# Attention and the first quarter of the output projection in one written order on five engines, with map sums and sub-norm roots on GpSimd

## The chip, the cores and the metric

The kernel runs on one core of one Trainium2 chip. The metric is the device time of one execution in microseconds, the median of several runs. The core has five engines that run side by side, each through its own list of instructions in order: TensorE (PE; its weight loads are shown as PEld), VectorE (DVE), ScalarE (ACT), GpSimd (POOL) and SyncE (SP), which here only issues DMA transfers. An instruction that waits for another engine or a transfer holds up everything behind it in its engine's list.

## What is computed

One layer of a diffusion backbone in fp32: 512 latent tokens and 256 context tokens of width 2048. The part that matters here:

```
p = modulate(rmsnorm(x)) @ w_in                       # one input projection for both mixers
q_da, k_da, v_da        = heads of p                  # 8 differential heads, two halves of 64
c_q, c_kv, k_rope       = rest of p                   # compressed inputs of 8 latent heads
w  = softmax(q1 k1^T) - lambda * softmax(q2 k2^T)     # differential head: two maps, 768 keys
o_da = rmsnorm_per_head(w @ v) * subln_w * (1 - lambda_init)
q, k, v = c_q @ w_uq, c_kv @ w_ukv                    # latent heads
o_mla = softmax([q_nope,q_rope] [k_nope,k_rope]^T * scale) @ v
x = x + g1 * (concat(o_da, o_mla) @ w_o)
x = x + g2 * conv_ffn(modulate(rmsnorm(x)))           # the longest stage, not touched here
out = rmsnorm(x) * final_w
```

## The kernel before

All matrix products are made in a split form: an fp32 operand is copied to a rounded high part (ScalarE, `sc.copy`) and a low part, the difference (VectorE, `ve.tensor_tensor`), and `mm3` (lines 101 to 106) adds three products high*high, high*low, low*high. Every weight block and every intermediate operand thus needs a ScalarE and a VectorE step before TensorE can use it.

Stages, in the order of the program: normalisation and modulation; the input projection (features, then values, line 483 on, whose results are split and written to DRAM by lines 496 to 498, the second half of them from GpSimd's queue); the eight differential heads (`da_head`, line 551); the eight latent heads (loop at line 657, with `latent_pair` at 591 projecting queries, keys and values for two heads); the output projection in four groups (g = 0 to 2 at line 735, the fourth in a later written order); the MLP; the final norm.

A differential head: `da_queries` (539) projects the head's queries, 48 matmuls of 512 columns, turns them by the rotary table (`apply_rope`) and stacks high and low parts. Keys and values come back from DRAM (554 to 558). For each of four query tiles and two maps `scores_softmax` (506) makes four matmuls into a two-bank score tile `s` (two buffers), VectorE takes the row maximum (512), ScalarE the exponent with its row sum (514). The two maps are joined: GpSimd scales the second map (567), VectorE scales the first and adds (568):

```
gp.tensor_scalar(out=ps[1], in0=ps[1], scalar1=rl[:, 1:2], scalar2=neglam, op0=ALU.mult, op1=ALU.mult)
ve.scalar_tensor_tensor(out=ps[0], in0=ps[0], scalar=rl[:, 0:1], in1=ps[1], op0=ALU.mult, op1=ALU.add)
```

`weighted_values` (517) then does six times: four transposes of the joined map into `pt`, high and low parts `wth` and `wtl` (line 80 and 81, by `split_tiles`), `mm3` into `po`; a copy (525) ends the head.

A latent head has 40 score matmuls, scales its map on VectorE (668) and uses the same `weighted_values`. `sub_norm` (646) is called once in each latent head for one stored differential head: load, square, a sum over partitions by a full fp32 matmul with ones (653), the root by `rstd` (157: two ScalarE and four VectorE steps), and a scaling (655).

What sets the order: the first stage and everything from the fourth projection group on stand in an order written out by hand (`tc.manual_schedule`). Between them, and so in all that is described here, the program gives operations and their dependences, and the framework's scheduler puts each engine's instructions in an order of its own; it mixes, for instance, the next head's query matmuls into the present head's scores, and the first output projection matmuls into the last latent head. Buffers come from pools; a tile that takes the place of an older one waits until that one's users are done.

Of the kernel before, what the change touches and what calls it, by code (L numbers as in the profile page):

```python
# [13 lines left out]
ALU = mybir.AluOpType  # L14
# [38 lines left out]
def layer_kernel(ctx: ExitStack, tc: tile.TileContext, small, rope, c_row, cc_row, x_t, ctx_t, ada, ada_k,  # L53
# [72 lines left out]
    ones32 = cst.tile([P, P], F32, name="ones32")  # L126
# [379 lines left out]
    def scores_softmax(mms, pool, tag, bufs, l):  # L506
        s = s_tile()
        for c0, c1 in ((0, T), (T, TT)):
            for i, (a, b) in enumerate(mms):
                pe.matmul(s[:, c0:c1], a, b[:, c0:c1], start=i == 0, stop=i == len(mms) - 1)  # L510
        m = sm.tile([P, 1], F32, tag="m", name=nm("m"), bufs=4)
        ve.tensor_reduce(out=m, in_=s[:, :TT], axis=AX.X, op=ALU.max, negate=True)
        p = pool.tile([P, TT], F32, tag=tag, name=nm(tag), bufs=bufs)
        sc.activation(p, s[:, :TT], AF.Exp, bias=m, accum_out=l)
        return p

    def weighted_values(pool, ws, v, dst, last=False):
        po = b_tile("po", 1)
        for kt in range(NKEY):
            pt = b_tile("f", 2) if last and kt % 3 else b_tile("pt", 1)  # L520
            for qt in range(NQT):
                pe.transpose(pt[:, qt * P:(qt + 1) * P], ws[qt][:, kt * P:(kt + 1) * P], ident)
            wth, wtl = split_tiles(pool, ("wth", "wtl"), [P, T], 2, pt)
            mm3(po, v(kt), (wth, wtl), kt == 0, kt == NKEY - 1)
        sc.copy(dst, po)


    da = tc.alloc_tile_pool(name="da", bufs=1, reuse_waits="tile")

# [6 lines left out]
    def da_rtmp():  # L536
        return da.tile([P, T], F32, tag="rt", name=nm("rt"), bufs=2)

    def da_queries(h):
        if h == 0:  # L540
            qs = [da.tile([P, T], F32R, tag=f"qs{i}", name=nm("qs"), bufs=2) for i in range(2)]
            for i in range(2):
                nc.sync.dma_start(qs[i].bitcast(F32), q0_d[i])
            return qs
        lat = b_tile("f", 2)
        feature(lat, None)
        q = da_rtmp()
        apply_rope(q, lat, da_rtmp)
        return stacked_queries(da, q, DA_SCALE)

    def da_head(h, qs):
# [5 lines left out]
        v = da.tile([P, 2, NKEY, P], F32R, tag="v", name=nm("v"), bufs=2)  # L557
        nc.sync.dma_start(v.bitcast(F32), v_d[h // 4][h % 4])
        ws = []
        for qt in range(NQT):  # L560
            c = slice(qt * P, (qt + 1) * P)
            l = sm.tile([P, 2], F32, tag="l", name=nm("l"), bufs=4)
            ps = [scores_softmax([(qs[i][:, c], ks[:, i]), (qs[i][:, c], kl[:, i])], da, f"p{i}", (8, 3)[i],
                                 l[:, i:i + 1]) for i in range(2)]
            rl = sm.tile([P, 2], F32, tag="rl", name=nm("rl"), bufs=4)
            ve.reciprocal(rl, l)
            gp.tensor_scalar(out=ps[1], in0=ps[1], scalar1=rl[:, 1:2], scalar2=neglam, op0=ALU.mult, op1=ALU.mult)
            ve.scalar_tensor_tensor(out=ps[0], in0=ps[0], scalar=rl[:, 0:1], in1=ps[1], op0=ALU.mult, op1=ALU.add)
            ws.append(ps[0])
        o = da.tile([P, T], F32, tag="o", name=nm("o"), bufs=2)  # L570
        weighted_values(da, ws, lambda kt: (v[:, 0, kt], v[:, 1, kt]), o)
        nc.sync.dma_start(o_d[h], o)

    for h in range(NH):
        da_head(h, da_queries(h))
    ap_.release()


    mc = tc.alloc_tile_pool(name="mc", bufs=1, side="right", reuse_waits="tile")

    def latents(src, width):
        hl = [mc.tile([P, width], F32R, name=nm("cn")) for _ in range(2)]
        for i in range(2):
            nc.sync.dma_start(hl[i].bitcast(F32), src[i])
        return hl

    cqn = [latents(d, T) for d in cq_d]
    ckvn = [latents(d, TT) for d in ckv_d]
    ma = tc.alloc_tile_pool(name="ma", bufs=1, side="right", reuse_waits="tile")

    def latent_pair(pr):

        pool = mb if pr % 2 else ma
        wh, wl = wblock(w_uqr[pr], 384)
        po = b_tile("f", 2)
        for j in range(3):
            mm3(po, (wh[:, j * P:(j + 1) * P], wl[:, j * P:(j + 1) * P]), cqn[j], j == 0, j == 2)
        qr = ma.tile([P, T], F32, tag="qr", name=nm("qr"), bufs=1)
        apply_rope(qr, po, lambda: ma.tile([P, T], F32, tag="rt", name=nm("rt"), bufs=2))
        qs = stacked_queries(pool, qr, MLA_SCALE, 1)  # L600
        qn, kn, vs = [], [], []
        qw = wblock(w_uqn[pr], 768)
        kw = wblock(w_ukv[pr])

        def queries_keys(i):
            po = b_tile("f", 2)
            for j in range(3):
                o = i * 384 + j * P
                mm3(po, [w[:, o:o + P] for w in qw], cqn[j], j == 0, j == 2)
# [804 lines left out]
```

## Time and profile before

| what | value |
|---|---|
| median of 3 runs | 2440.16 us (2439.8 to 2440.46) |
| span of the profiled execution | 2439.6 us |
| TensorE busy | 2367.0 us, 97% |
| VectorE busy | 1735.5 us, 71% |
| ScalarE busy | 1117.0 us, 46% |
| GpSimd busy | 220.2 us, 9% |
| mean granted TensorE clock | 0.992 |
| first query matmul of the differential heads | 473.99 us after the span's start |
| last matmul of the first projection group | 919.3 us |

The profile is one execution, and its span lies 0.56 us under the median of the runs. A row of a stretch gives its length and then, for PE, PEld, DVE, ACT and POOL, busy time and number of instructions, then the granted clock, the share of the DMA engines and GB/s. A row of the order of time gives start, duration, engine, line, output<-inputs, sizes, and in brackets the idle time before it with what ended it. A row of groups gives line, engine, names, shapes, count, busy time, mean ns of one, and the idle time before. A wait row gives who waited for whom: total us, times, longest.

### The profile page before, as it was taken

The page shows a single profiled execution, that of the slowest core. Times are in us where ns is not written, and L with a number is a line of the kernel's source. Part 1 is how long each engine was busy: PE and PEld are TensorE (multiplying, and loading weights), DVE is VectorE, ACT ScalarE, POOL GpSimd, SP SyncE. Part 2 cuts the span into 40 slices and gives each one's busy share as a digit, 9 for nine tenths or more (in the row PEclk, how much of TensorE's full clock was granted, in tenths as well). Part 3 has the DMA queues.
Part 4 walks back from the last instruction along what each step waited for, and adds up shares of the span by engine and source line. Part 5 has one row for each costly group of instructions (what it writes and reads, how often), then busy time and mean ns, then how long its engine had stood idle before and what let it go on. Part 6 is the DMA issues. An engine that isn't in the chain of part 4 may idle for free.

```text
span 2439.6 us, 32889 instructions
## 1 busy us (share of the span) xinstructions
PE 2367.0 (97%) x12758; PEld 1978.4 (81%) x12758; DVE 1735.5 (71%) x2316; ACT 1117.0 (46%) x1696; POOL 220.2 (9%) x244
## 2 busy tenths in 40 slices
PE   6999999999999999999999999999999999999998
PEld 3678877777777778889888888888888888888888
DVE  6668876388868878378667676767666666666667
ACT  4432121155646542245445454545454545454545
POOL 0000000121100003100111111111111111111110
PEclk9999999999999999999999999999999999999999
DMA  8758889555411149423555555555555565556573
GB/s 300 279 211 309 327 319 330 181 166 144 127 59 44 44 161 349 146 87 113 147 130 143 134 140 137 137 139 136 141 134 143 132 143 132 141 135 140 133 188 111
DMA packets 130707, 403.32 MB, mean 165 GB/s; under 512 B 14323, under 2 KB 25075, under 8 KB 122099
## 3 DMA queue, kind: packets, MB, share of 16 engines
q1 hardware_dynamic: 104118, 350.87, 43.7%
q0 software_dynamic: 25280, 49.30, 11.6%
q8 instruction: 100, 1.64, 0.3%
q10 hardware_dynamic: 1152, 1.05, 0.1%
q14 instruction: 57, 0.47, 0.1%
HBM read 331.68 MB, written 69.48 MB: 164 GB/s over the span
## 4 chain that ended last, share of the span: by engine, by line
PE 76%; DVE 8%; issue 7%; ACT 4%; DMA 3%; POOL 2%; SPq 0%; DVEq 0%; ACTq 0%; POOLq 0%
PE y L1133 11%; PE b L105 9%; PE b L104 9%; PE b L106 9%; PE z L1133 5%; PE y L1135 5%; PE s L104 3%; PE s L105 3%; PE s L106 3%; PE z L1135 3%; PE s L510 3%; PE x L1133 2%; DMA ada<-in_ada 2%; PE b L206 1%; PE f L104 1%
## 5 line engine op out<-in xcount | busy, mean ns | idle before, releaser
L989 DVE TENSOR_TENSOR wl<-wr,wh 128x1024 fp32r<-128x1024 f32 x144 | 176.4, 1225 | 157.8 <-ACT wh L981 157.1
L981 ACT CAST wh<-wr 128x1024 fp32r<-128x1024 f32 x144 | 151.0, 1049 | 234.0 <-PE b L105 118.5
L104 PE MATMUL b<-ah,wh 128*128 128x512 f32 (+1 forms) x664 | 256.8, 387 | 0.0
L105 PE MATMUL b<-al,wh 128*128 128x512 f32 (+1 forms) x664 | 256.7, 387 | 0.0
L106 PE MATMUL b<-ah,wl 128*128 128x512 f32 (+1 forms) x664 | 255.9, 385 | 0.0
L1154 POOL DMA_DIRECT2D x_d<-xs x160 | 139.6, 1004 | 1162.6 <-ACT xs L1153 1159.3
L989 DVE TENSOR_TENSOR wl<-rb,wh 128x1024 fp32r<-128x1024 f32 x123 | 150.0, 1220 | 126.9 <-ACT wh L981 126.8
L981 ACT CAST wh<-rb 128x1024 fp32r<-128x1024 f32 x123 | 129.2, 1050 | 185.7 <-PE b L105 116.1
L989 DVE TENSOR_TENSOR wl<-ws,wh 128x1024 fp32r<-128x1024 f32 x123 | 150.1, 1220 | 90.1 <-ACT wh L981 90.1
L80 ACT CAST wh<-wr 128x1024 fp32r<-128x1024 f32 (+3 forms) x102 | 99.2, 972 | 217.0 <-PE b L106 62.1
L171 DVE CUSTOM_DVE_ANT_0 ada<-ada,cb,smt 128x2048 f32<-128x2048 f32 x64 | 152.5, 2382 | 54.6 <-DMA ada<-in_ada 54.2
L981 ACT CAST wh<-ws 128x1024 fp32r<-128x1024 f32 x123 | 128.2, 1043 | 130.3 <-DVE ws L943 44.3
L1133 PE MATMUL y<-a2k,wh 128*128 128x512 f32 x656 | 164.0, 392 | 0.0
L81 DVE TENSOR_TENSOR wl<-wr,wh 128x1024 fp32r<-128x1024 f32 (+3 forms) x102 | 116.9, 1146 | 62.1 <-ACT wh L80 61.7
L104 PE MATMUL b<-a2k,wh 128*128 128x512 f32 (+1 forms) x376 | 141.6, 377 | 5.9 <-ACT a2k L838 4.3
L106 PEld LDWEIGHTS b<-ah,wl 128*128 128x128 f32 x664 | 124.8, 188 | 25.7
L104 PEld LDWEIGHTS b<-ah,wh 128*128 128x128 f32 x664 | 125.1, 188 | 22.9
L105 PEld LDWEIGHTS b<-al,wh 128*128 128x128 f32 x664 | 125.1, 188 | 21.9
L105 PE MATMUL b<-a2k,wh 128*128 128x512 f32 (+1 forms) x376 | 140.8, 374 | 0.0
L106 PE MATMUL b<-a2k,wl 128*128 128x512 f32 (+1 forms) x376 | 140.0, 372 | 0.0
L1133 PEld LDWEIGHTS y<-a2k,wh 128*128 128x128 f32 x656 | 118.6, 189 | 21.6
L1133 PE MATMUL y<-b2k,wh 128*128 128x512 f32 x410 | 107.8, 393 | 0.0
(454 smaller groups left out, 5757.2 us busy)
## 6 DMA issues: line engine op xcount, KB each, us to landing
ada<-in_ada SPq DMA_DIRECT2D x64, 1024.0 KB, 6.4
rb<-in_w_up SPq DMA_DIRECT2D x123, 512.0 KB, 4.3
wr<-in_w_dn SPq DMA_DIRECT2D x88, 512.0 KB, 4.3
x_d<-xs POOLq DMA_DIRECT2D x160, 256.0 KB, 6.0
wr<-in_w_up SPq DMA_DIRECT2D x53, 512.0 KB, 4.2
wr<-in_w_f SPq DMA_DIRECT2D x34, 512.0 KB, 6.0
ada<-in_ada SPq DMA_DIRECT2D x32, 512.0 KB, 6.4
adak<-in_ada_k SPq DMA_DIRECT2D x32, 512.0 KB, 6.3
```

Of the source, the lines that this page charges most:

```text
L80: sc.copy(dst_h, src)
L81: ve.tensor_tensor(dst_l, src, dst_h.bitcast(F32), op=ALU.subtract)
L104: pe.matmul(out, st[0], mv[0], start=start, stop=False, **kw)
L105: pe.matmul(out, st[0], mv[1], start=False, stop=False, **kw)
L106: pe.matmul(out, st[1], mv[0], start=False, stop=stop, **kw)
L171: ve.tensor_tensor_reduce(out=junk, in0=w, in1=vec, op0=ALU.mult, op1=ALU.add, scale=1.0, scalar=col("b_ada", j), accum_out=dst[:, j:j + 1])
L510: pe.matmul(s[:, c0:c1], a, b[:, c0:c1], start=i == 0, stop=i == len(mms) - 1)
L981: sc.copy(t, raw[:, k * n_:k * n_ + n_])
L989: ve.tensor_tensor(t, raw[:, k * n_:k * n_ + n_], hi[k].bitcast(F32), op=ALU.subtract)
L1133: pe.matmul(o, w[j][0], hs[j], start=start and j == 0, stop=False, skip_group_check=True)
L1135: pe.matmul(o[:, h0], w[j][1], hs[j][:, h0], start=False, stop=j == 7, skip_group_check=True)
L1154: gp.dma_start(x1_d[dt], x, accum_op=ALU.add)
```

## The change

The differential heads, the latent heads and the first projection group (g = 0) are recorded as steps with a time (`at(t, f)`), sorted by it and issued under `tc.manual_schedule` for all five engines, GpSimd included. The times only decide the order in each engine's list. `SPANS` gives each head its length: 17, six of 23.2 and 19 us for the differential heads, 21 and 22.8 in turn (the last 16) for the latent ones; `BASE` are their starts, and the last projection step stands at 399.1.

- Within a head, scores are spread evenly; the next head's query matmuls run from 6 us before the head at an even pace; the weighted values of head h run inside head h + 1, one key block every 3.05 us (2.5 to 3.3 in the latent heads).
- The joining of the maps: GpSimd scales the second map as before, ScalarE scales the first (`da_first`), GpSimd adds them (`da_sum`). VectorE no longer takes part.
- `sub_norm`: the square is split into two parts (ScalarE, GpSimd) and summed by two matmuls with fp32r ones; the root's four VectorE steps and the last scaling go to GpSimd (five steps, in `power`) and ScalarE (`root`, and the scaling by `subs`).
- Pools: a new pool `dp` holds maps, transposed parts, values and head outputs for both kinds of heads, opened ahead of `da`; the values of a head are two tiles; stored outputs live in a pool `mq` that takes the place of `da`.
- The first projection group and its weight blocks, with the split of the 16 head outputs, follow in the same order; the loads of the next group's first blocks too. The modulation rows of the groups g = 1 and 2 (`next_gemv`) are as before, behind the written order.

The core of the diff (`...` marks what is left out):

```diff
+    def at(t, f, *a):
+        plan.append((t, len(plan), f, a))
...
+    def block(t, key, src, cols=1024):
+        at(t - 12, fetch, key, src, cols)
+        at(t - 3.4, high_part, key)
+        at(t - 2.2, low_part, key)
...
-    def scores_softmax(mms, pool, tag, bufs, l):
+    def softmax(t, key, mms, tag, bufs, l, tall):
+        at(t, score, key, mms)
+        at(t + tall + 0.1, peak, key)
+        at(t + tall + 1.2, exponent, key, tag, bufs, l)
+        return t + tall + 2.4
...
+    def weighted_values(t, h, step, dst, done=None):
         for kt in range(NKEY):
+            t0 = t + step * kt
+            at(t0, turn, h, kt)
+            split_at(t0 + 0.55, (dp, dp), ("wth", "wtl"), [P, T], 2, lambda: live["pt", h],
+                     lambda hl, kt=kt: live.__setitem__(("wt", h, kt), hl), width=0.7)
+            at(t0 + step - 0.2, values, h, kt)
...
+    SPANS = [17, 23.2, 23.2, 23.2, 23.2, 23.2, 23.2, 19] + [21, 22.8, 21, 22.8, 21, 22.8, 21, 16]
+    BASE = [sum(SPANS[:i]) for i in range(17)]
...
+    def da_first(h, qt):
+        p = live[("s", h, qt, 0), "p"]
+        sc.mul(p, p, live["rl", h, qt][:, 0:1])
+
+    def da_sum(h, qt):
+        p, p1 = (live[("s", h, qt, i), "p"] for i in range(2))
+        gp.tensor_tensor(out=p, in0=p, in1=p1, op=ALU.add)
+        live["w", h, qt] = p
...
+    FIRST = -9.0
+    at(FIRST, first_queries)
+    at(FIRST, load_keys, 0)
...
+    for h in range(NH):
+        b, step = BASE[h], SPANS[h] / 8
         for qt in range(NQT):
+            for i in range(2):
+                t = softmax(b + (2 * qt + i) * step, ("s", h, qt, i), ...)
+            at(t, da_norm, h, qt)
+            at(t + 0.2, da_second, h, qt)
+            at(t + 0.2, da_first, h, qt)
+            at(t + 1.5, da_sum, h, qt)
+        at(b + 2, load_values, h)
+        if h + 1 < NH:
+            at(b + 1, load_keys, h + 1)
+            f0, pace = (FIRST, 0.75) if h == 0 else (b - 6, (SPANS[h] - 0.3) / 16)
...
+            for kt in range(KT):
+                at(f0 + pace * kt, da_feature, h + 1, kt)
...
+        weighted_values(BASE[h + 1] + 4.8, h, 3.05 if h < 7 else 2.7, ...)
...
+        def low_():
+            live["sub", "lo"] = tile_("s2", F32R)
+            gp.tensor_tensor(out=live["sub", "lo"], in0=live["sub", "sq"], in1=live["sub", "hi"].bitcast(F32),
+                             op=ALU.subtract)
+
+        def total():
+            po = live["sub", "po"] = b_tile("f", 2)
+            for i, g in enumerate(("hi", "lo")):
+                pe.matmul(po, onesr, live["sub", g], start=i == 0, stop=i == 1)
+
+        def root():
+            po, s1, rs = live["sub", "po"], tile_("sq"), tile_("sr")
+            sc.activation(rs, po, AF.Ln, bias=epst, scale=1.0 / P)
+            sc.activation(s1, po, AF.Identity, bias=epst, scale=1.0 / P)
+
+        def power():
+            rs, s1, t2 = live["sub", "sr"], live["sub", "sq"], tile_("s2")
+            sc.activation(rs, rs, AF.Exp, scale=-0.5)
+            sc.mul(oraw[h], oraw[h], subs)
+            gp.tensor_tensor(out=t2, in0=rs, in1=rs, op=ALU.mult)
+            gp.tensor_tensor(out=t2, in0=t2, in1=s1, op=ALU.mult)
+            gp.tensor_scalar(out=t2, in0=t2, scalar1=-0.5, scalar2=1.5, op0=ALU.mult, op1=ALU.add)
+            gp.tensor_tensor(out=rs, in0=rs, in1=t2, op=ALU.mult)
+            gp.tensor_tensor(out=oraw[h], in0=oraw[h], in1=rs, op=ALU.mult)
+
+        at(t, load)
+        at(t + 3.5, square)
+        at(t + 4.3, high_)
+        at(t + 5, low_)
+        at(t + 8, total)
+        at(t + 8.8, root)
+        at(t + 10.3, power)
...
+    tw = BASE[15] + 14.8
+    at(tw - 2.4, open_projection)
+    for kb in range(8):
+        t = tw + 8 * 0.9 * kb
+        at(t - 14, wo_fetch)
...
+                at(t + 0.9 * order, project_at, kb, j, i)
...
+    with tc.manual_schedule(engines={mybir.EngineType.PE, mybir.EngineType.Activation, mybir.EngineType.DVE,
+                                     mybir.EngineType.SP, mybir.EngineType.Pool}):
+        run_plan()
```

More of the change, by code (lines that the diff above doesn't have):

```diff
@@ L510, in scores_softmax, with peak @@
                 pe.matmul(s[:, c0:c1], a, b[:, c0:c1], start=i == 0, stop=i == len(mms) - 1)
[L511 to L518, printed above, removed]
-        for kt in range(NKEY):
[L520 to L525, printed above, removed]
+    def peak(key):
+        m = live[key, "m"] = sm.tile([P, 1], F32, tag="m", name=nm("m"), bufs=4)
+        ve.tensor_reduce(out=m, in_=live[key][:, :TT], axis=AX.X, op=ALU.max, negate=True)
@@ new lines, in turned, with first, second @@
+    def turned(t, src, tmp, keep):
+        def first():
+            first.q, first.t = tmp(), tmp()
+            ve.tensor_tensor(first.q, src(), ropet[:, 0, :], op=ALU.mult)
+            ve.stream_shuffle(first.t, src(), mask=[i ^ 16 for i in range(32)])
+        def second():
+            ve.tensor_tensor(first.t, first.t, ropet[:, 1, :], op=ALU.mult)
+            ve.tensor_tensor(first.q, first.q, first.t, op=ALU.add)
+            keep(first.q)
+        at(t, first)
+        at(t + 1.5, second)
```

453 lines of the change are left out of this document (317 added, 136 removed).

## The prediction

> **What bounds the kernel now.** I read the page first, then busy time by stretch over the part that the change rewrites (about 474 to 920 us), then the waits of TensorE in it, and last the order of time, because the first three don't agree with it.
>
> ```profile
> span 2439.6 us, 32889 instructions
> PE 2367.0 (97%) x12758; PEld 1978.4 (81%) x12758; DVE 1735.5 (71%) x2316; ACT 1117.0 (46%) x1696; POOL 220.2 (9%) x244
> 500.00:540.00 40.00, 39.51 (x197) 31.02 (x198) 38.20 (x55) 26.12 (x50) 8.85 (x8) 1.00 0.45 125
> 900.00:940.00 40.00, 40.00 (x178) 33.12 (x177) 31.62 (x27) 9.92 (x11) 9.48 (x7) 1.00 0.92 342
> sum 460.00, PE 436.53 PEld 345.29 DVE 369.63 ACT 245.37 POOL 54.42; mean PE 31.18 PEld 24.66 DVE 26.40 ACT 17.53 POOL 3.89
> PE pt L522 <- DVE p L568: 5.4, 7, 2.1
> ```
>
> Columns after the stretch: its length, then PE, PEld, DVE, ACT, POOL. TensorE is the bound in every stretch; in the differential heads VectorE (38.2 of 40) stands right behind it. The waits name little (5.4 us in all for the weighted sum of the two maps, line 568), and the sum over 480 to 940 leaves only 23.5 us of TensorE idle. That is misleading, as the order of time shows:
>
> ```profile
> 546.91 0.39 PE L106 MATMUL f<-a2k,wl 128*128 128x512 f32 x1
> 547.14 0.40 PE L104 MATMUL f<-a2k,wh 128*128 128x512 f32 x1
> 548.06 0.60 PE L522 MATMUL pt<-ident,p 128*128 128x128 f32 x4
> 548.42 0.48 PE L106 MATMUL f<-a2k,wl 128*128 128x512 f32 x1
> 548.73 0.40 PE L104 MATMUL f<-a2k,wh 128*128 128x512 f32 x1
> 563.80 0.28 PE L510 MATMUL s<-ks,qs 128*128 128x256 f32 x1
> 563.92 0.28 PE L510 MATMUL s<-klz,qs 128*128 128x256 f32 x1
> 572.80 0.59 ACT L525 COPY o<-po 128x512 f32<-128x512 f32 x1 [0.63 <-PE po L106]
> 676.40 0.58 ACT L525 COPY o<-po 128x512 f32<-128x512 f32 x1 [1.96 <-PE po L106]
> 738.77 0.58 ACT L525 COPY b2k<-po 128x512 f32<-128x512 f32 x1 [1.67 <-PE po L106]
> 834.82 0.58 ACT L525 COPY b2k<-po 128x512 f32<-128x512 f32 x1 [1.68 <-PE po L106]
> ```
>
> A 512-column matmul starts 0.23 after the one before it but counts as busy for 0.39, so a wait of up to 0.16 doesn't show as idle. By starts, a 512-column matmul costs 0.23, a 256-column one 0.115 (0.12 in the row), and a group of four transposes 0.36 plus 0.08 on the matmul behind it, 0.44.
>
> A differential head with the next head's queries has 48 + 16 + 18 = 82 matmuls of 512 columns, 16 of 256 and 6 groups of transposes: 18.9 + 1.8 + 2.6 = 23.3 us. The output copies at 572.80 and 676.40 are four heads apart: 25.9 each, so 2.6 us per head are lost. A latent head has (mean of a pair) 57.5 of 512, 44 of 256, 6 groups and one full fp32 sum (0.85, below): 13.2 + 5.1 + 2.6 + 0.85 = 21.8; the copies at 738.77 and 834.82, four heads apart, give 24.0: 2.2 lost. This is what an order can win: at most some 8 x 2.6 + 8 x 2.2 = 38 us.
>
> **The start.** Here the change costs time.
>
> ```profile
> 473.99 0.39 PE L104 MATMUL f<-a2k,wh 128*128 128x512 f32 x1
> 476.07 0.76 POOL L498 DMA_DIRECT2D v_d<-kh  x1 [0.48 <-ACT kh L80]
> 477.44 0.75 POOL L498 DMA_DIRECT2D v_d<-kl  x1 [0.61 <-DVE kl L81]
> 479.99 0.59 ACT L80 CAST kh<-b 128x512 fp32r<-128x512 f32 x1 [2.23 <-DMA v_d<-kh]
> 484.14 0.69 DVE L81 TENSOR_TENSOR kl<-b,kh 128x512 fp32r<-128x512 f32 x1 [5.63 <-DMA v_d<-kl]
> 488.31 0.75 POOL L498 DMA_DIRECT2D v_d<-kl  x1 [0.52 <-DVE kl L81]
> 488.95 0.76 PE L510 MATMUL s<-ks,qs 128*128 128x512 f32 x1 [4.60 <-DMA ks<-k_d]
> 488.00:492.00 4.00, 2.87 (x7) 2.11 (x8) 2.00 (x3) 0.00 (x0) 3.48 (x5) 0.50 1.01 358
> 492.00:496.00 4.00, 4.00 (x16) 3.32 (x16) 2.73 (x6) 2.93 (x5) 0.19 (x1) 0.73 1.06 333
> klz<-k_d SPq DMA_DIRECT2D x16, 192.0 KB, 5.6
> ```
>
> Before, 45 query matmuls of head 1 run from 473.99 while the values are split and written; then TensorE waits for the keys until 488.95. In the changed program's order, the pools opened anew put the query accumulator f into the bank of the fifth value tile, so the first query matmul waits for the fifth low half (the DVE row at 484.14), and the low key tile klz lies where the value halves lay, so its load waits for the last value write (the POOL row at 488.31), with every later SP load queued behind it: the other half of the keys, head 1's keys, the values, the weights of head 2.
>
> The fifth low half waits for the landing of the third pair's write. The rows give two landings: 476.07 to 479.99 is 3.9 us, 477.44 to 484.14 is 6.7, the second beside SP's key and value loads, which now come later. The writes start about 1 us earlier, since one weight cast no longer stands between the copies. So f starts at 476.4 + 3.9 + 0.7 = 481, at worst 484. The clock was granted at 0.50 and 0.73 in the two stretches after the present wait, which costs 4 x 0.50 + 4 x 0.27 = 3.1 us; 36 query matmuls stand before the first score: 36 x 0.23 + 3.1 = 11.4, done at 492.4 to 495.4. Beside it, the last write is issued at about 483 to 486, lands 3.9 to 6.7 later, and klz lands 5.6 after that: 492.5 to 498.3. First score: 493, bounds 492 to 499, against 488.95, with nine query matmuls (2.1 us) fewer behind it, but with the slow clock already paid for. The start costs 4.0 + 2.1 - 3.1 = 3 us.
>
> **Work of each engine in a head.** The change takes line 568 off VectorE, and gives the scaling of the first map to ScalarE and the sum to GpSimd.
>
> ```profile
> L512 DVE TENSOR_REDUCE m<-s 128x1 f32<-128x768 f32 x96 | 90.5, 950 | 14.6 <-PE s L510 14.3
> L81 DVE TENSOR_TENSOR wtl<-pt,wth 128x512 fp32r<-128x512 f32 x91 | 62.5, 687 | 21.5 <-ACT wth L80 20.7
> L514 ACT ACTIVATE p<-s,m 128x768 f32<-128x768 f32 x64 | 57.8, 903 | 44.9 <-DVE m L512 41.6 <-issue 1.7 <-ACT p L514 1.0
> L568 DVE SCALAR_TENSOR_TENSOR p<-p,rl,p 128x768 f32<-128x768 f32 x32 | 32.5, 1015 | 9.5 <-POOL p L567 9.0
> L80 ACT CAST wh<-wr 128x768 fp32r<-128x768 f32 x4 | 3.4, 839 | 4.4 <-PE f L105 4.4
> L567 POOL TENSOR_SCALAR p<-p,rl,neglam x32: 980/984/2285, 496.9 to 675.1; 128x768 f32<-128x768 f32 x32
> L705 POOL TENSOR_TENSOR ss<-ss,sq x11: 1285/1729/2769, 919.3 to 1011.5; 128x512 f32<-128x512 f32 x11
> 733.98 1.02 PE L653 MATMUL f<-sq,ones 128*128 128x512 f32 x2
> 735.06 0.39 PE L106 MATMUL po<-wth,mvl 128*128 128x512 f32 x1
> ```
>
> VectorE: from its busy rate it needs 38.2 / 40 x 25.9 = 24.7 per head now; less four of 1.015 it needs 20.7 in a TensorE head of 23.3. ScalarE: 26.1 / 40 x 25.9 = 16.9, plus four scalings of 768 columns at 0.84, 20.3. GpSimd: no 768-column sum is in the trace; by the 512-column row one takes 1.285 x 1.5 = 1.93 undisturbed, at most 2.77 x 1.5 = 4.15; I take 1.93 since the row's slow cases ran beside other two-input work. Four of them and four of 0.98: 11.6. All three stay under TensorE. The last sum of a head has its slot 24.9 us after the head's first and ends at 26.8, the transposes that read it stand at 28.0: 1.2 us of room, gone at 4.15 (then each head waits 1 us for it).
>
> The sub-norm root moves from VectorE to GpSimd and ScalarE: five GpSimd steps and a low half of about 1.29 each, 7.7 of a latent head's 21.4; nobody waits for its result before the output projection. Its sum of squares becomes two matmuls of 0.23 instead of one in full fp32, which with the matmul behind it took 733.98 to 735.06, so 1.08 - 0.23 = 0.85: 8 x 0.39 = 3 us saved. The step that squares a stored head has its slot 3.5 us after the load, and loads land later than that (5.6 in the row of klz): ScalarE stands up to 2.1 us, eight times, with the next copies and exponents queued behind it, inside its own slack. The output projection's first quarter is already dense before (40.00 of 40), and the scheduler already put it beside the last head: nothing for that.
>
> **The sum.** TensorE's work from the first query matmul to the end of the first quarter is, in the changed order, 1276 of 512 columns, 480 of 256 and 96 groups: 293.5 + 55.2 + 42.2 = 390.9; without the 36 matmuls, 382.6 are left at the first score. Head 0 has 11.6 of it in a slot of 17, held by the chain score, peak, exponent through two score buffers: 5.4 idle. Of the lost 2.6 and 2.2 per head I leave half (a value that has just arrived still delays the matmul that waits for it): 8 x 1.3 + 8 x 1.1 = 19.2. So the quarter ends at 493 + 382.6 + 5.4 + 19.2 = 900.2. Before, it ends here:
>
> ```profile
> L106 PE MATMUL s<-a2k,wl x53: 389/389/389, 882.8 to 919.3; 128*128 128x512 f32 x53
> ```
>
> 919.3 + 0.4 = 919.7, so 19.5 us are won. Behind it the code is as before and TensorE dense; the 16 modulation rows that began inside the first quarter now begin after it, where VectorE has room. The span is 2439.6, the median of the runs 2440.16: 2440.16 - 19.5 = 2421 (rounded).
>
> **The rivals.** *Denser:* a quarter of the loss stays and the start meets its lower bound: 492 + 382.6 + 5.4 + 9.6 = 889.6, 30 us won, 2410. For it: in the written order every operand is due before its matmul by the rows' durations, 0.3 to 2.4 us ahead. *Idle is what the busy rows say:* only 23.5 us, 4.6 of them at the start; half of the other 19 is 9.5, plus 3 from the sums, less a start at its bound of 499 (9): 3.5 won, 2437, no change. Against it: the head's pace. *Slower, GpSimd against VectorE:*
>
> ```profile
> 628.46 0.67 DVE L151 TENSOR_TENSOR rt<-rt,ropet 128x512 f32<-128x512 f32 x1
> 628.64 1.34 POOL L567 TENSOR_SCALAR p<-p,rl,neglam 128x768 f32<-128x768 f32 x1 [3.31 <-DVE rl L566]
> 629.16 1.36 DVE L152 TENSOR_TENSOR rt<-rt,rt 128x512 f32<-128x512 f32 x1
> ```
>
> GpSimd's 0.98 became 1.34 beside a VectorE step with two SBUF inputs, and the next such step took 1.36 instead of 0.67, ending 0.54 after GpSimd let go at 629.98. Six such steps stand in a differential head (two weight low halves, two rotary, two stacked). With GpSimd busy half of the time, each waits some 0.5: 3 us, VectorE at 23.7, about TensorE's pace: inside the half that I left. If each waits for a whole sum, VectorE has 20.7 + 6 x 1.93 = 32.3 a head against my 24.6: 7 x 7.7 = 54 lost, 2475. It decides where the wait per step passes (24.6 + 2.8 - 20.7) / 6 = 1.1 us. The Trainium skill, "SBUF — State Buffer", section "SBUF: two separate sides", states such a rule: a GpSimd operation and a VectorE one with two SBUF inputs share a port pair, held for the whole instruction, and the loser fully blocks; by it alone the worst case is the whole wait. The three rows agree with it.
>
> **How the numbers follow.** Chances: the forecast 0.50, denser 0.26, no change 0.09, slower 0.15. A measurement of this kernel tells about 0.2% (4.9 us) from no change. Faster takes in the first two, 0.76. The range runs from 2407 (3 under the denser case) to 2440 (the no-change case with its start), leaving out the slower one and little below.
>
> **What would show it.** Right: first score near 493 after a TensorE gap of 7 us; output copies 24.6 us apart in the differential heads, about 22.5 in the latent ones; VectorE under 22 in 24.6; last first-quarter matmul near 900. Wrong: copies 26 or more apart with TensorE waiting for line 700's sums or VectorE steps over 1.2 us beside them, or a first score past 499.

## The result, and the profile after

| kernel | median us | runs | profiled execution, span us |
|---|---|---|---|
| before | 2439.98 | 2438.03 to 2440.46 | 2439.6 |
| changed | 2501.91 | 2497.34 to 2505.28 | 2500.5 |

The changed kernel is slower: the ratio is 1.0246, 95% interval 1.0228 to 1.0265, 62 us, where 2421 was forecast and 2407 to 2440 given as range.

First the head of the page of the changed kernel, then its busy time by stretch, in the columns that the prediction explained (the sum is over 480 to 940 us, as for the kernel before):

```profile
span 2500.5 us, 33000 instructions
PE 2380.5 (95%) x12758; PEld 1989.3 (80%) x12758; DVE 1700.9 (68%) x2244; ACT 1155.7 (46%) x1752; POOL 330.7 (13%) x324
```

```profile
500.00:540.00 40.00, 33.55 (x148) 25.04 (x146) 24.84 (x36) 23.62 (x42) 16.93 (x12) 0.91 0.26 76
...
sum 460.00, PE 396.57 PEld 312.23 DVE 286.03 ACT 261.68 POOL 151.47; mean PE 33.05 PEld 26.02 DVE 23.84 ACT 21.81 POOL 12.62
```

No engine is busy throughout. In the stretch 500 to 540 TensorE fell from 39.51 busy of 40 to 33.55 and VectorE from 38.20 to 24.84, and ScalarE stands at 23.62: all three wait for somebody. The order of time gives the last value product of the stage ahead, the start, the copies that end a head, and the last matmul of the first projection group:

```profile
470.66 0.39 PE L106 MATMUL b<-wh,c2k 128*128 128x512 f32 x1
477.41 0.80 PE L104 MATMUL f<-a2k,wh 128*128 128x512 f32 x1 [6.36 <-DVE kl L81]
...
488.58 0.39 PE L566 MATMUL s<-ks,qs 128*128 128x512 f32 x1
...
572.99 0.57 ACT L605 COPY o<-po 128x512 f32<-128x512 f32 x1
...
603.71 0.57 ACT L605 COPY o<-po 128x512 f32<-128x512 f32 x1
...
634.47 0.57 ACT L605 COPY o<-po 128x512 f32<-128x512 f32 x1
...
779.09 0.58 ACT L605 COPY or<-po 128x512 f32<-128x512 f32 x1
...
883.95 0.58 ACT L605 COPY or<-po 128x512 f32<-128x512 f32 x1
...
979.15 0.39 PE L106 MATMUL s<-a2k,wl 128*128 128x512 f32 x1
```

A differential head takes 30.7 us (603.71 - 572.99) against 24.6 forecast. Before it took 25.9 by the four heads that the prediction read, and 23.8 by the first seven copies, the measure of the table below. A latent head takes (883.95 - 779.09) / 4 = 26.2 against 24.0 before and 22.5 forecast. The first group ends at 979.15; it was 919.3 before and 900 in the forecast. Of the 60.9 us between the two spans 59.9 lie ahead of this point; behind it the kernels differ by 1 us.

TensorE's own waits from 480 to 980 us name who was late, ScalarE and VectorE in turn:

```profile
PE po L104 <- ACT wth L545: 21.0, 25, 3.4
PE po L105 <- DVE wtl L552: 20.1, 39, 1.3
...
PE pt L587 <- POOL p L700: 1.0, 1, 1.0
```

TensorE waits 41 us for high and low parts of transposed maps, though both engines that make them are only some 60% busy in the stretch above. For GpSimd's sums (line 700) it waits once, 1.0 us.

Why they are late is seen in the order of time of ScalarE and VectorE (`...` stands for lines of TensorE but one, of GpSimd, and of the small reciprocal):

```profile
614.68 0.69 DVE L552 TENSOR_TENSOR wtl<-pt,wth 128x512 fp32r<-128x512 f32 x1 [1.54 <-ACT wth L545]
...
615.29 0.95 DVE L570 TENSOR_REDUCE m<-s 128x1 f32<-128x768 f32 x1
...
616.10 0.60 PE L587 MATMUL pt<-ident,p 128*128 128x128 f32 x4
616.33 0.90 ACT L574 ACTIVATE p<-s,m 128x768 f32<-128x768 f32 x1 [1.68 <-DVE m L570]
...
617.13 0.19 ACT L574 ACTIVATION_READ_ACCUMULATOR p<-s,m 128x1 f32 x1
617.22 0.58 ACT L545 CAST wth<-pt 128x512 fp32r<-128x512 f32 x1
...
617.69 0.95 ACT L696 ACTIVATE p<-p,rl 128x768 f32<-128x768 f32 x1
...
617.83 0.69 DVE L552 TENSOR_TENSOR wtl<-pt,wth 128x512 fp32r<-128x512 f32 x1 [0.31 <-ACT wth L545]
...
618.44 0.95 DVE L570 TENSOR_REDUCE m<-s 128x1 f32<-128x768 f32 x1
...
619.42 0.90 ACT L574 ACTIVATE p<-s,m 128x768 f32<-128x768 f32 x1 [0.78 <-DVE m L570]
```

The maximum ends at 616.24, and only then does ScalarE, which had idled 1.68 us, begin the exponent that stands next in its list. The high part behind it has its transposed block at 616.70 (616.10 + 0.60) but starts at 617.22, when the exponent is done. VectorE, with the low part next in its list, waits for that high part, and the next maximum stands behind the low part. This turn, from maximum to maximum, is 3.15 us. Of the eight turns of a head three are like it (3.09 to 3.15); the others have other steps of the same lists in them and take 2.7 to 5.3, 30.8 in all. The chain of waits shows them (shares of one head, 604.94 to 635.73, then some of its pieces: start, us, step):

```profile
by line: DVE m L570 21.4%; ACT p L574 14.0%; issue 13.1%; DVE wtl L552 9.9%; PE s L566 6.5%; ACT wh L523 6.2%; DVE rt L661 5.1%; ACT wth L545 4.7%; DVE wl L529 4.1%; PE po L105 3.2%; DVE rt L662 2.3%; DVE qs L676 2.2%; PE f L106 2.2%; ACT q
604.94 0.97 DVE m L570
605.93 0.99 ACT p L574 x2
606.93 0.95 ACT wh L523
607.90 1.23 DVE wl L529
609.13 0.88 DVE m L570
...
612.20 0.96 DVE m L570
...
623.26 0.50 PE po L105
...
625.13 0.71 PE s L566 x4
...
634.41 1.29 PE s L566 x4
```

For the first 18 us of the head the chain goes from VectorE to ScalarE and back and never touches TensorE. After that it passes through TensorE twice (623.26 to 625.84, and 632.73 to 635.70). A weight block's high and low part (606.93 to 609.13) lie in it like the rest. The theory that was tested: the written lists of ScalarE and VectorE form a **ring**, in which each step waits for the last step of the other engine, and a head lasts as long as the way round.

### The profile page after: what moved, and what is told of

It is laid out like the page before. It is cut to its first block, busy times and chain, and to the rows that moved or that the text cites. A ratio compares the mean times of both kernels' runs of the same rounds, so it can differ in the third digit from the quotient of the medians.

```text
span 2500.5 us, 33000 instructions
## 1 busy us (share of the span) xinstructions
PE 2380.5 (95%) x12758; PEld 1989.3 (80%) x12758; DVE 1700.9 (68%) x2244; ACT 1155.7 (46%) x1752; POOL 330.7 (13%) x324
## 3 DMA queue, kind: packets, MB, share of 16 engines
q0 software_dynamic: 25280, 49.30, 11.1%
## 4 chain that ended last, share of the span: by engine, by line
PE 83%; DVE 9%; ACT 5%; issue 2%; DMA 1%; DVEq 0%; POOL 0%; ACTq 0%
PE y L1471 12%; PE b L105 10%; PE b L104 10%; PE b L106 10%; PE z L1471 6%; PE y L1473 6%; PE s L104 3%; PE s L106 3%; PE s L105 3%; PE z L1473 3%; PE s L566 3%; PE x L1471 2%; DVE m L570 2%; DVE wtl L552 1%; ACT p L574 1%
## 5 line engine op out<-in xcount | busy, mean ns | idle before, releaser
L172 DVE CUSTOM_DVE_ANT_0 ada<-ada,cb,smt 128x2048 f32<-128x2048 f32 x64 | 153.2, 2397 | 48.6 <-DMA ada<-in_ada 48.4
L80 ACT CAST wh<-wr 128x1024 fp32r<-128x1024 f32 (+1 forms) x68 | 66.4, 976 | 175.2 <-PE b L106 75.7
L106 PEld LDWEIGHTS b<-ah,wl 128*128 128x128 f32 x664 | 124.8, 188 | 25.7
L574 ACT ACTIVATE p<-s,m 128x768 f32<-128x768 f32 x96 | 86.6, 903 | 95.7 <-DVE m L570 95.7
L570 DVE TENSOR_REDUCE m<-s 128x1 f32<-128x768 f32 x96 | 91.3, 951 | 43.4 <-PE s L566 43.0
```

The costliest lines, as they stand in the source:

```text
L106: pe.matmul(out, st[1], mv[0], start=False, stop=stop, **kw)
L172: ve.tensor_tensor_reduce(out=junk, in0=w, in1=vec, op0=ALU.mult, op1=ALU.add, scale=1.0, scalar=col("b_ada", j), accum_out=dst[:, j:j + 1])
L570: ve.tensor_reduce(out=m, in_=live[key][:, :TT], axis=AX.X, op=ALU.max, negate=True)
L574: sc.activation(p, live[key][:, :TT], AF.Exp, bias=live[key, "m"], accum_out=l())
```

## The experiments

Rivals of the ring were the shared **port** (GpSimd's sums hold up VectorE, the prediction's slower rival) and the **clock** (it is 0.91 in the stretch above, 1.00 before). The results in one table; the pace of a differential head is the mean over the first seven copies, that of a latent pair over the second to the sixth:

| kernel | median us | ratio to before, 95% | diff. head us | latent pair us |
|---|---|---|---|---|
| before | 2439 to 2442 | 1 | 23.8 | 48.0 |
| changed | 2501.91 | 1.0246 [1.0228, 1.0265] | 30.7 | 52.4 |
| low part later | 2539.75 | 1.0412 [1.0392, 1.0432] | 35.3 | 52.5 |
| paired | 2484.14 | 1.0191 [1.0174, 1.0208] | 27.7 | 51.7 |
| only TensorE as written | 2490.65 | 1.0212 [1.0197, 1.0228] | 28.0 | 53.3 |
| all but TensorE as written | 2468.36 | 1.0116 [1.0099, 1.0132] | 29.4 | 46.3 |
| no written order | 2439.21 | 0.9988 [0.9979, 0.9997] | 24.6 | 45.1 |
| changed, maps joined on VectorE | 2490.18 | 1.0212 [1.0194, 1.0229] | 29.1 | 52.5 |
| changed, sub-norm as before | 2524.82 | 1.0337 [1.0322, 1.0352] | 30.5 | 58.0 |
| before, maps joined on GpSimd | 2452.90 | 1.0049 [1.0035, 1.0062] | 23.6 | 48.4 |
| before, root on GpSimd | 2450.29 | 1.0040 [1.0027, 1.0053] | 23.7 | 48.1 |
| other lists | 2435.60 | 0.9976 [0.9964, 0.9987] | 27.0 | 43.0 |
| other lists, worked out again | 2424.98 | 0.9927 [0.9913, 0.9940] | 25.7 | 44.1 |
| the same, maps joined on VectorE | 2420.48 | 0.9906 [0.9893, 0.9920] | 25.5 | 43.5 |

**One number of the written times: the low part later.**

```diff
-                       lambda hl, kt=kt: live.__setitem__(("wt", h, kt), hl), width=0.7)
+                       lambda hl, kt=kt: live.__setitem__(("wt", h, kt), hl), width=1.4)
```

> The changed kernel with one number of the written times changed: the low part of a transposed key block (line 552) stands 1.4 us instead of 0.7 us behind its high part, so that more of them come to stand behind the next row maximum (line 570) in VectorE's list. Work, engines and buffers are the same. Theory 1 (ring): ScalarE's and VectorE's written lists make them take turns, one step of one engine always waiting for the last step of the other, so a head lasts as long as the chain through both lists; in the changed kernel that is 30.75 us from copy to copy (the copies of line 605 at 572.99, 603.71, 634.47). One more 0.95 us maximum between high and low part in most of the six key blocks makes the ring longer: copies 32 to 34 us apart, 2510 to 2525 us in all. Theory 2 (port): VectorE is held up by GpSimd's sums (line 700); no number of instructions changes, so 2502 within 5 us. Theory 3 (clock): the TensorE clock of 0.91 in this stretch is the cause and the waits follow from it: no change, 2502 within 5 us.

Measured: 2539.75 us, the first six copies 35.7 to 36.3 us apart. The same instructions, with the low parts later in VectorE's list and nothing else moved, cost 38 us; from 480 to 980 us TensorE's wait for low parts went from 20.1 to 65.0 us. The ring is borne out in its direction and was sized too low; the port and the clock, which expected no change, are out as the main cause.

**Three numbers: maximum and high part side by side, exponent and low part side by side.**

```diff
-        weighted_values(BASE[h + 1] + 4.8, h, 3.05 if h < 7 else 2.7, ...
+        weighted_values(BASE[h + 1] + (6.05 if h < 7 else 4.8), h, 2.9 if h < 7 else 2.7, ...
-                       lambda hl, kt=kt: live.__setitem__(("wt", h, kt), hl), width=0.7)
+                       lambda hl, kt=kt: live.__setitem__(("wt", h, kt), hl), width=0.9)
```

> The changed kernel with three numbers of the written times changed, differential heads only: key blocks of a head go in the rhythm of the next head's scores (2.9 us instead of 3.05), starting 6.05 us instead of 4.8 us into it, and the low part stands 0.9 us behind the high part. Now a row maximum (VectorE) and a high part (ScalarE) stand side by side, and then an exponent (ScalarE) and a low part (VectorE), so that neither list waits for a step that the other has only just begun. Theory 1 (ring): the copies of line 605 come 26 to 28.5 us apart instead of 30.75 in the six full differential heads, 15 to 28 us won: 2474 to 2487 us. Theory 2 (port) and theory 3 (clock as the cause): the same instructions on the same engines, 2502 within 5 us.

Measured: 2484.14 us, the first five copies 27.5 to 27.6 us apart. This is as the ring says, and 18 us are won back with no step taken away.

**The written order for some engines only.** The set of engines in `tc.manual_schedule` is cut (names shortened here); the framework's scheduler orders the others' lists.

```diff
-    with tc.manual_schedule(engines={PE, Activation, DVE, SP, Pool}):
+    with tc.manual_schedule(engines={PE}):                           # only TensorE as written
+    with tc.manual_schedule(engines={Activation, DVE, SP, Pool}):    # all but TensorE as written
+    run_plan()                                                       # no written order
```

> The changed kernel with the written order kept for TensorE alone (the set of engines of the written order is cut to PE); ScalarE, VectorE, GpSimd and SyncE get their order from the framework's scheduler again, as before the change. Same instructions on the same engines. Theory 1 (ring, made by the order of ScalarE's and VectorE's lists): copies 26 to 28.5 us apart in the differential heads, and 40 us of the stage's loss of some 62 us mostly gone: 2450 to 2480 us. Theory 2 (port): the sums are still GpSimd's, so 2490 or more. Theory 4 (TensorE's own written order waits for operands that no order of the others can bring earlier): copies still 30 us or more apart, 2495 to 2510 us.

> The changed kernel with the written order kept for ScalarE, VectorE, GpSimd and SyncE, and TensorE's list left to the framework's scheduler: the counterpart of the run with only TensorE's list as written (2490.65 us); with all lists free it is 2439.21 us, with all as written 2501.91 us. If the ring runs through ScalarE's and VectorE's lists alone, it stays: 2490 to 2505 us, copies 30 us apart. If TensorE's list is a part of it, so that a transposition or a product that stands behind a matmul that isn't ready closes it, then either half of the written order alone costs a part: copies 28 to 29.5 us apart, 2465 to 2490 us.

> The changed kernel with no written order at all in this stretch: all five engines' lists come from the framework's scheduler, as before the change; the two moves to GpSimd and the new buffers stay. If the written order is the whole of the loss beyond the moves (theory 1), this is the kernel before plus the two moves, which alone cost 12.4 and 9.8 us: 2450 to 2468 us. If the steps themselves or their buffers (the single transposed buffer, the shared pools) make the waits whatever the order: 2480 us or more.

Measured: 2490.65, 2468.36 and 2439.21 us. Without any written order the changed kernel is as fast as the one before, faster than I had expected: the whole loss is the order, and not the steps, the engines or the buffers. But the theory was too narrow. With the other four lists free, TensorE's list alone keeps 51 of the 63 us, where I had expected most of it to go. Its waits are the same two as in the changed kernel, 38.5 us in all against 41.1; first its rows, then two of the run with TensorE's list free:

```profile
PE po L105 <- DVE wtl L552: 22.8, 32, 3.8
PE po L104 <- ACT wth L545: 15.7, 16, 2.4
```

```profile
PE pt L587 <- POOL p L700: 18.0, 7, 4.7
...
PE po L104 <- ACT wth L545: 4.2, 5, 0.9
```

With TensorE's list free, little of it waits for high and low parts; it now waits for the joined maps. The latent heads are quick (46.3 a pair), the differential heads are not (29.4). So either half of the order is enough to make a loss: TensorE's list in both kinds of heads, the others' in the differential heads. I read this as a ring through three lists, and the chain above does enter TensorE's list twice a head. But no run shows which of TensorE's steps closes it, and the four other lists were not tried one by one.

**The maps joined on VectorE again, in the written order.**

```diff
-        gp.tensor_tensor(out=p, in0=p, in1=p1, op=ALU.add)
+        ve.scalar_tensor_tensor(out=p, in0=p, scalar=live["rl", h, qt][:, 0:1], in1=p1, op0=ALU.mult, op1=ALU.add)
...
-            at(t + 0.2, da_first, h, qt)
```

> The changed kernel with the two maps joined as before the change: one VectorE step instead of ScalarE's scaling and GpSimd's sum; the written order is kept. Theory 1 (ring): ScalarE's scaling of the first map and GpSimd's sum hardly stand in the chain of waits between 600 and 640 us, so copies 30 to 31.5 us apart and 2497 to 2508 us. Theory 2 (port): 32 sums of 1.83 us on GpSimd that hold up VectorE go; by the 1.1 us for each that the prediction's rival took, 32 x 1.1 = 35 us are won: 2460 to 2480 us.

Measured: 2490.18 us, between the two, 12 us less than the changed kernel. The groups of VectorE's steps (500 to 740 us) show a part of it, first in the changed kernel, then here:

```profile
L552 DVE TENSOR_TENSOR wtl<-pt,wth 128x512 fp32r<-128x512 f32 x46 | 31.6, 686 | 23.1 <-ACT wth L545 23.1
...
L676 DVE SCALAR_TENSOR_TENSOR qs<-rt,qs 64x512 fp32r<-64x512 f32 x14 | 11.0, 787 | 5.9 <-ACT qs L672 5.7
L661 DVE TENSOR_TENSOR rt<-rt,ropet 128x512 f32<-128x512 f32 x7 | 10.6, 1518 | 0.0
L662 DVE TENSOR_TENSOR rt<-rt,rt 128x512 f32<-128x512 f32 x7 | 6.9, 980 | 0.2
```

```profile
L552 DVE TENSOR_TENSOR wtl<-pt,wth 128x512 fp32r<-128x512 f32 x48 | 33.0, 687 | 16.2 <-ACT wth L545 16.1
...
L676 DVE SCALAR_TENSOR_TENSOR qs<-rt,qs 64x512 fp32r<-64x512 f32 x14 | 9.6, 687 | 0.4
L662 DVE TENSOR_TENSOR rt<-rt,rt 128x512 f32<-128x512 f32 x8 | 5.5, 693 | 0.3
L661 DVE TENSOR_TENSOR rt<-rt,ropet 128x512 f32<-128x512 f32 x8 | 5.5, 683 | 0.0
```

The steps that read two operands from SBUF are stretched beside GpSimd's sum: 1518 - 683, 980 - 693 and two times 787 - 687 make 1.3 us a head. The low part, which reads one operand from PSUM, has 686 and 687. So the port is there. The head became 1.5 us shorter, but not by the port alone. The turn that holds the rotary steps, from maximum to maximum, fell from 5.26 to 4.56 us. The turn behind it fell from 4.60 to 3.77, and all of that lies in its matmuls, from the product that waits for the low part to the next maximum: 3.00 us in the changed kernel (632.73 to 635.73), where they run at half rate, and 2.16 here (631.66 to 633.82), where they don't. So about half of the 1.5 us is the port and half the clock, each about a tenth of the 6.9 us that a head lost (30.7 - 23.8).

**The sub-norm as before, in the written order** (one fp32 matmul, the root and the scaling on VectorE, at the written times of the changed steps).

```diff
-            gp.tensor_tensor(out=t2, in0=rs, in1=rs, op=ALU.mult)
-            gp.tensor_tensor(out=t2, in0=t2, in1=s1, op=ALU.mult)
...
+            ve.scalar_tensor_tensor(out=t2, in0=rs, scalar=-0.5, in1=rs, op0=ALU.mult, op1=ALU.mult)
+            ve.tensor_tensor(t2, t2, s1, op=ALU.mult)
...
```

> The changed kernel with the sub-norm as before the change (one full fp32 matmul with ones, the root's four VectorE steps and the last scaling on VectorE), at the written times of the changed kernel's steps; the joining of the maps and the order of all else stay. Theory 1 (ring): five more VectorE steps of 0.68 us behind each other, one of them waiting for ScalarE, stand in the middle of VectorE's written list in each latent head, so the ring there grows: copies of a latent pair 53 to 57 us apart instead of 52, 2505 to 2525 us. Theory 5 (GpSimd's chain is what costs, as the 10 us of the kernel before with this move alone suggest): 2485 to 2497 us.

Measured: 2524.82 us, latent pairs 58.0 us, a little more than the ring was expected to make of them. Five more steps in VectorE's list lengthen it in the direction expected.

**Each move alone, on the kernel before.**

```diff
-            ve.scalar_tensor_tensor(out=ps[0], in0=ps[0], scalar=rl[:, 0:1], in1=ps[1], op0=ALU.mult, op1=ALU.add)
+            sc.mul(ps[0], ps[0], rl[:, 0:1])
+            gp.tensor_tensor(out=ps[0], in0=ps[0], in1=ps[1], op=ALU.add)
```

> The kernel before with only the joining of the two maps changed as in the change: ScalarE scales the first map, GpSimd adds; the order is the scheduler's. If the engine move itself is good: VectorE, at 24.7 us of the 25.9 us of a differential head before, loses four steps of about 1 us in each head, and up to 1 us for each of eight heads is won: 2430 to 2440 us. If the port is what counts (theory 2): 32 sums of 1.83 us on GpSimd stretch the rotary steps beside them (lines 661 and 662 of the changed kernel together 1.1 us longer in each head than before), and the sum of GpSimd lies in the way from map to transposition: 2440 to 2465 us.

> The kernel before with only the sub-norm changed as in the change: the square split in two parts and summed by two matmuls, the root's four VectorE steps and the last scaling on GpSimd and ScalarE; the order is the scheduler's. The prediction put 8 x 0.39 = 3 us for the matmuls; VectorE also loses five steps of 0.68 to 0.74 us in each latent head (rows of 5.5 us for 8), 28 us in all, in a stretch in which it is 80% busy. If VectorE's load counts there: 2425 to 2437 us. If only the matmuls count: 2437 us. If GpSimd's longer chain (five steps of 1.3 us) delays the last heads: 2440 us or more.

Measured: 2452.90 and 2450.29 us, both slower, as the second case of the first expectation and the last case of the other had it. With the maps joined on GpSimd TensorE's transposes wait longer for their map, 11.1 us instead of the 5.4 that the prediction showed:

```profile
PE pt L522 <- POOL p L569: 11.1, 11, 2.3
```

The rotary steps aren't stretched here (685 and 814 ns), so that part of the port's expectation is wrong. Other steps with two operands in SBUF are: from 500 to 740 us the low half of a 1024-column weight block takes 1417 ns instead of 1216 (11 of them), one of 384 columns 950 instead of 543 (3), a stacking step 871 instead of 734 (14), some 5 us in all. How much of this and of the longer wait is in the 12 us isn't settled. The 10 of the root lie in the last latent heads: counted from the last value product, the fifth latent copy comes 1.3 us earlier than before and the last one 11.2 us later. Which step makes them isn't settled either. The two don't add up either: both moves with the changed kernel's steps and buffers, in the scheduler's order, cost nothing (2439.21).

**Other lists.** The same steps, in a fixed order that was worked out from the rows' durations.

```diff
-        for _, _, f, a in sorted(plan, key=lambda x: x[:2]):
+        for i in ORDER:              # a written list of the 1454 steps (1422 in the third run)
+            _, _, f, a = plan[i]
             f(*a)
```

> The changed kernel with the same steps, engines, tiles and loads, but the steps between the first query matmul and the end of the first projection group stand in another order, written out as a list of numbers: each engine takes as its next step one whose operands will be there first, worked out once from the durations of the rows of the changed kernel (maximum 0.87 us from start to start, exponent 0.99, high part 0.54, low part 0.58, sum 1.85, matmul 0.2155). TensorE's order changes too, because the run with only TensorE's order kept as written (2490.65 us) showed that the order of the other lists alone wins back only 11 of the 62 us. SyncE's order is as written. Theory 1 (ring: in-order lists that take turns, TensorE's among them): the copies of the differential heads come 22 to 25.5 us apart instead of 30.75, those of the latent heads 46 us or less for a pair instead of 52, and 50 to 100 us of the changed kernel's time go: 2400 to 2450 us, so at or below the kernel before. Theory 2 (port): GpSimd's sums are as many, and what they hold up stays: 2470 us or more. Theory 3 (clock): the clock of the stretch does not rise and copies stay 28 us or more apart, 2470 us or more.

> As the run with all lists put in another order (2435.6 us), worked out anew with two things that its trace showed: from 660 to 700 us, between the two kinds of heads, its copies were 39.9 us apart and TensorE's clock 0.86, since no step of the latent heads could stand before one of the differential heads in any list; here they can overlap. And a TensorE step after more than 1.3 us of idling counts double for 3.3 us, as the pitch of 0.43 us does in the traces. Theory 1: the gap between the kinds of heads 30 us or less; 2422 to 2434 us. If the transition is bound by the loads of the latents: 2435 us or more.

> As the run before it in this list, and with the maps joined by one VectorE step as before the change; the order worked out in the same way. VectorE has 20.7 + 4 x 1 = 25 us of steps in a head of 23 to 26 us, as before the change, but no GpSimd sum of 1.83 us lies between exponent and transposition and no rotary step is held up (1.28 and 1.07 us instead of 0.68 and 0.70 in the run with other lists). If those count more than VectorE's load: 2418 to 2432 us. If VectorE's load binds: 2436 us or more.

Measured: 2435.60, 2424.98 and 2420.48 us. The first wins back 66 us with every step as in the change; the third is the fastest kernel of the study, 0.9% under the one before, with an interval of 0.8 to 1.1%. Its busy time by stretch, in which TensorE is the bound again:

```profile
540.00:580.00 40.00, 39.76 (x206) 33.19 (x205) 37.19 (x55) 25.73 (x46) 6.96 (x7) 1.00 0.44 138
...
660.00:700.00 40.00, 36.31 (x207) 31.01 (x208) 32.86 (x53) 25.33 (x52) 8.27 (x9) 0.96 0.15 54
...
sum 460.00, PE 447.13 PEld 374.29 DVE 365.61 ACT 263.50 POOL 112.59; mean PE 37.26 PEld 31.19 DVE 30.47 ACT 21.96 POOL 9.38
```

Against the run before it this one differs in the joining and in the order worked out for it. The two together are worth 4.5 us, and the intervals of the two ratios overlap a little, so that VectorE's one step is better than ScalarE's and GpSimd's two isn't shown. Between the kinds of heads (660 to 700) something is still lost: one copy there comes 38.4 us after the last.

## Why the prediction was wrong

**The step that failed** is the term "Of the lost 2.6 and 2.2 per head I leave half", 19.2 us. By the prediction's own sum it measured 979.15 + 0.4 - 488.58 - 382.6 - 5.4 = 103 us. It took for granted that a written order loses no more than the scheduler's, since "every operand is due before its matmul by the rows' durations, 0.3 to 2.4 us ahead". That check held each operand's written time against that of its matmul, one dependency at a time, and each engine's total against TensorE's ("All three stay under TensorE"). Both sums are near: VectorE and ScalarE are busy some 60% of the time. But a written list isn't only a time. A step that is late by a little holds back all behind it, and here those are the operands of the other engine, whose lateness comes back. Between maximum and exponent the plan has 1.1 us for a step of 0.95, between high and low part 0.7 for one of 0.58, and several steps stand at the same time on one engine; the way round a head came to 30.7 us. That the order made the loss is shown (2439.21 us without it), and that single places in it do (38 us lost, 18 won back); that the steps close a ring is read from the chain of waits. I should have followed one step through the lists of three engines until it came back to itself. The Trainium skill, "PSUM — Partial Sum Buffer", section "Engine vs sequencer instructions", states that ScalarE's and VectorE's queues are strictly first in, first out, and that matmuls start in program order. The rows agree: a high part whose block was there at 616.70 started at 617.22, behind an exponent.

**Reading of the kernel before:** the loss that busy rows hide was there to be won: the last kernel of the study, with TensorE's steps of the change, ends 21 us under the kernel before. But 25.9 us was the pace of four heads; over the first seven copies it is 23.8, only 0.5 over the 23.3 of work, and more was lost elsewhere, as in the 43.8 us between the last differential copy and the first latent one (694.94 to 738.77). That the last kernel lies near the forecast says nothing for the forecast, since the changed kernel's own order doesn't win it.

**The start:** the mechanism was right, and the size near. The query matmuls waited for the fifth low half as named (6.36 us, 7 forecast). That the first score came at 488.58, under the bound of 492, is mostly luck: the stage ahead, whose code is the same, ended 3.1 us earlier in this profile. Its last value product is the row at 470.66 above; before it was this one:

```profile
473.76 0.39 PE L106 MATMUL b<-wh,c2k 128*128 128x512 f32 x1
```

In the profiles of this study it lies anywhere from 469.3 to 477.8. Counted from it, the first score came after 17.9 us (19.2 forecast, 15.2 before), with nine query matmuls fewer behind it. In the prediction's own terms the start cost 2.7 + 2.1 - 3.1 = 1.7 us, where 3 were forecast.

**The slower rival, GpSimd against VectorE:** the mechanism was right, the price too high. The condition, over 1.1 us of wait for each of six steps, wasn't met: 1.3 us in a whole head, on the rotary and stacking steps, none on the weight low halves. Undoing the sums won 12 us where the rival had 54, and only about half of that was the port. So my two signs of error, TensorE waiting for line 700's sums and VectorE steps over 1.2 us beside them, showed 1.0 us once and one step of 1.5 us a head: the copies were "26 or more apart" for a reason that I hadn't listed.

**Engine loads:** GpSimd's sum was put at 1.93 us and took 1.83; VectorE in 500 to 540 has 24.84 / 40 x 30.7 = 19.1 us a head (20.7 forecast), ScalarE 18.1 (20.3). **Sub-norm:** 3 us were forecast. In the written order the move is worth 23 us (2524.82 - 2501.91), which the theory puts down to VectorE's shorter list; on the kernel before it costs 10. **First quarter:** nothing was lost there; from the last head's copy to its end are 27.9 us (951.23 to 979.15), before 33.8 (885.48 to 919.28).

## What to carry to other kernels

When a scheduler's order is replaced by a written one, follow the chain of waits through the lists of all engines together: a plan in which each operand is due in time and each engine has room can still make engines take turns. A sign in the profile is that no engine is busy throughout and that the waits of two engines name each other. That heads are equally long is no such sign: four in a row are here (30.72 to 30.77 us), but so are three of the fastest kernel (23.66 to 23.73 us). Put side by side in time steps of two engines that don't feed each other (here maximum and high part, then exponent and low part: 18 us won back), and test the order by moving one number: here 0.7 us in a written time cost 38 us.

## What the hardware showed

TensorE fell to half its rate after short stops. In the changed kernel, rows of TensorE in the order of time:

```profile
601.97 0.51 PE L105 MATMUL po<-wtl,vh 128*128 128x512 f32 x1 [1.33 <-DVE wtl L552]
602.31 0.40 PE L106 MATMUL po<-wth,vl 128*128 128x512 f32 x1
602.55 0.40 PE L104 MATMUL f<-a2k,wh 128*128 128x512 f32 x1
...
603.42 0.63 PE L566 MATMUL s<-ks,qs 128*128 128x512 f32 x1
603.85 0.63 PE L566 MATMUL s<-klz,qs 128*128 128x512 f32 x1
...
605.13 0.63 PE L105 MATMUL f<-a2k,wh 128*128 128x512 f32 x1
```

A stop of 1.33 us, then 512-column matmuls 0.23 apart, and from 603.4 on 0.43 apart for some 3 us; four differential heads in a row have this after such a stop. The Trainium skill, "TensorE: Matmul & The Clock Gate", section "What's actually happening", has the clock halved after an idle window of about 3.4 us; no stop in the 6 us ahead of this was longer than 1.33 us, so these rows don't fit that figure. No run here shows what decides it: a fifth head has the half rate after a stop of 0.96 us, and with the maps joined on VectorE a stop of 1.06 us is followed by matmuls 0.23 apart. The low clock is a part of the loss (0.8 of the 30.7 us of a head, by the turn compared above). That it made most of it is ruled out by a run in which it rose and the loss stayed: with the maps joined on VectorE, in the written order, it was 1.00 from 540 to 660 us and a head there still took 29.2. One of its stretches, which has TensorE busy 35.26 of 40:

```profile
580.00:620.00 40.00, 35.26 (x174) 27.14 (x173) 28.93 (x42) 19.88 (x39) 5.90 (x6) 1.00 0.47 142
```
